# A hybrid encoder layer on one core: a column sum queued later, and the first half's final norm on GpSimd and ScalarE

## The chip, the cores and the metric

The kernel runs on one core of a Trainium2 chip. The metric is the device time of one execution in microseconds. The core's engines are TensorE (PE; its weight loads are PEld), VectorE (DVE), ScalarE (ACT), GpSimd (POOL) and SyncE (SP). Each engine takes its own instructions strictly in order, and an instruction that has to wait holds everything behind it in its queue. In this kernel all loads and stores are issued from SP's queue.

## The reference

One layer and a final norm on x of 2048 frames x 1024 channels, float32. What is computed, cut to its core:

```python
h = rmsnorm(x, norm_mix_w)
proj = h @ w_in                              # 1024 -> 5648 columns
y_a = u_b * causal_dwconv(u_c * u_h, w)      # short convolution, width 3
y_b = rmsnorm(ssd_scan(silu(conv4(xbc)), softplus(dt), ...) * silu(z))
x = x + concat(y_a, y_b) @ w_out             # 2048 -> 1024
h = rmsnorm(x, norm_mlp_w)
hid = square(relu(h @ w_up))                 # 1024 -> 4096
x = x + hid @ w_down                         # 4096 -> 1024
out = x * rsqrt(mean(x * x) + eps) * final_norm_w
```

## The kernel before

Channels lie on the 128 partitions, frames along the free dimension. A float32 operand is split into a rounded part and a remainder (`hi` and `lo`, both in TensorE's fp32r format), and each product is made of three matmuls: hi by hi, hi by lo, lo by hi. So every weight and every activation passes through one cast (ScalarE, L100 for weights, L368 for activations) and one subtraction (VectorE, L101 and L369).

The projections in, up and down use a two-by-two block scheme with seven products instead of eight: `b11, t1, t2, b21, t3, b22, t4`, in this order, one after the other (the function `chain`). A step of that order takes about 19 us. The products add up in PSUM: b11, t2, t3 and t4 in the tile px, t1 and b22 in py, b21 in pw. After t1, t2, b21, t3, b22 and t4 the sum so far is read out (in the down projection by L1109, which adds it to a result tile), and TensorE goes on into px for t3 only when VectorE has read t2's sum, and for t4 only when it has read t3's.

The scheme needs sums of weight blocks. `combine` (L246) makes them for the next step while the present one runs: from two raw tiles r0 and r1 it splits r0, makes s12 (its first half by the addition L252, its second by a subtraction L229), splits s12, makes s34 by two subtractions, splits s34, and splits half of r1. In the first half of the projection in, and in the MLP's first half, s12 and s34 are also stored, to be loaded again in the second half. The raw tiles come by DMA, the loads being issued at the start of a step.

The order in which an engine's instructions stand is not the program's order alone: a scheduler puts them in order by priority and by when it takes their operands to be ready. `tc.issue_after(ins)` puts all instructions of a block behind `ins` on its engine. `kept` tiles and raw activations share small pools: `raw` (tag `uraw`) has four buffers for the reloaded activations `rh` and for the tiles `lf` of the final norm.

The frames are worked in two halves of 1024. In the down projection the first half is done some steps before the second, and from there on `finish_first` makes its final norm beside the second half's matmuls: for each of two blocks of 512 frames it loads eight channel tiles in pairs (`lf`), squares each pair on ScalarE (L1232), adds the squares on VectorE (L1234, L1237), makes the inverse root (`parts`, `whole`, with a reciprocal at L184), loads the pairs again, multiplies each tile by its weight column and by the inverse root in one VectorE instruction (L1248), and stores the pair. It moves on by one such piece after the products b11, t2 and t3 of a step. The second half's norm at the kernel's end (`norm_out`) does two of its tiles per three on VectorE, and one with the weight on ScalarE (L1205) and the inverse root on GpSimd (L1206).

Of the kernel before, what the change touches and what calls it, by code (L numbers as in the profile page):

```python
# [40 lines left out]
def trunk(ctx: ExitStack, tc: tile.TileContext, x, w_in, w_dt, w_out, w_up, w_down, cvec, hrow, out):  # L41
# [56 lines left out]
    def split_w(raw, eng):  # L98
        hi, lo = wtile(raw.shape[-1])
        nc.scalar.copy(hi, raw)  # L100
        eng.tensor_tensor(out=lo, in0=raw, in1=hi.bitcast(F32), op=ALU.subtract)  # L101
        return hi, lo

    def split_src(src):
        k = src.shape[1]
# [105 lines left out]
    class Seven:  # L211
# [35 lines left out]
        def combine(self, r0, r1, kept=None):  # L247
            w = r0.shape[-1] // 2
            a, b = slice(0, w), slice(w, 2 * w)
            yield split_w(r0, nc.vector)  # L250
            s12 = self.sumtile("s12")[:, 0 : 2 * w]
            nc.vector.tensor_tensor(out=s12[:, a], in0=r1[:, a], in1=r1[:, b], op=ALU.add)  # L252
            self.sub(s12[:, b], s12[:, a], r0[:, a])
            if kept is not None:
                nc.sync.dma_start(kept[:, 0], s12)
            yield split_w(s12, nc.vector)
            s34 = self.sumtile("s34")[:, 0 : 2 * w]
            self.sub(s34[:, a], r0[:, a], r1[:, a])
            self.sub(s34[:, b], r0[:, b], s12[:, b])
            if kept is not None:  # L260
                nc.sync.dma_start(kept[:, 1], s34)
            yield split_w(s34, nc.vector)
            yield split_w(r1[:, b], nc.vector)

        def chain(self, groups, ws, ahead, evict, after):
# [615 lines left out]
    class Mlp(Seven):  # L881
# [336 lines left out]
        def finish_first(self):  # L1218

            for bb in range(NBB):  # L1220
# [9 lines left out]
                for d in range(0, KD, 2):  # L1230
                    t = load(d)
                    nc.scalar.activation(t, t, AF.Square)  # L1232
                    if d == 0:
                        nc.vector.tensor_tensor(out=acc, in0=t[:, 0], in1=t[:, 1], op=ALU.add)  # L1234
                    else:
                        for i in range(2):
                            nc.vector.tensor_tensor(out=acc, in0=acc, in1=t[:, i], op=ALU.add)  # L1237
                    yield
                st = self.rstd()
                st.parts(acc)  # L1240
# [4 lines left out]
                for d in range(0, KD, 2):  # L1245
                    t = load(d)
                    for i in range(2):
                        nc.vector.scalar_tensor_tensor(  # L1248
                            out=t[:, i], in0=t[:, i], scalar=col(C_NFIN, d + i), in1=r, op0=ALU.mult, op1=ALU.mult
                        )  # L1250
                    nc.sync.dma_start(out[bb, :, d : d + 2], t)
                    yield

# [488 lines left out]
```

## Time and profile before

| | |
|---|---|
| median of the runs shown | 2623.73 us (2623.39 to 2628.8, three runs) |
| the profiled execution | 2627.32 us, of which the span from first to last instruction is 2625.6 us |
| granted TensorE clock, mean | 0.997 |
| TensorE busy | 2601.6 us, 99% |
| VectorE busy | 1917.3 us, 73% |
| ScalarE busy | 1468.0 us, 56% |
| GpSimd busy | 58.1 us, 2% |

A busy time is the time in which the engine had an instruction under way. A wait row reads: who waited, for which instruction, total in microseconds, times, longest. A timeline row reads: start and duration in microseconds, engine, source line, operation, result and operands by the program's names, shapes; in square brackets how long the engine was idle before it, and what ended that. Lines of the order are lines of the program, not times. The program's stages follow each other: projection in to about 930 us, projection out with the scan beside it to about 1390, up projection to about 1980, down projection to about 2570, then the last products and the second half's norm.

### The profile page before, as it was taken

How to read it: one execution, taken by the hardware profiler on the slowest of the kernel's cores; microseconds unless marked ns; L12 is line 12 of the kernel's file. 1: busy time of each engine (PE TensorE's matmuls, PEld its weight loads, DVE VectorE, ACT ScalarE, POOL GpSimd, SP SyncE). 2: the span in 40 equal slices, each digit the busy share in tenths (PEclk: the TensorE clock that was granted, in tenths of full speed). 3: DMA queues.
4: the chain of work that ended last, by engine and by line, in shares of the span. 5: the costliest groups of instructions: out<-in, count | busy, mean ns of one | idle time of the engine just before them, and what ended most of it. 6: DMA issues, size and time to landing. Idle time of an engine off the chain costs nothing.

```text
span 2625.6 us, 33818 instructions
## 1 busy us (share of the span) xinstructions
PE 2601.6 (99%) x12139; PEld 2141.9 (82%) x12139; DVE 1917.3 (73%) x2631; ACT 1468.0 (56%) x2230; POOL 58.1 (2%) x99
## 2 busy tenths in 40 slices
PE   9999999999999999999999999999999999999998
PEld 7788888788888888888888888888888888888887
DVE  7877877777778777778677775744448887888985
ACT  7654345776667666768335555755556444444533
POOL 1010000000000000000000000000000000000001
PEclk9999999999999999999999999999999999999998
DMA  4545745644555578877656786765557654665762
GB/s 155 194 172 181 278 143 194 208 156 164 170 165 173 167 270 257 272 221 230 206 196 237 263 314 235 280 212 193 197 192 254 194 174 153 217 200 180 244 201 69
DMA packets 252169, 536.98 MB, mean 205 GB/s; under 512 B 26208, under 2 KB 93024, under 8 KB 252000
## 3 DMA queue, kind: packets, MB, share of 16 engines
q1 hardware_dynamic: 251856, 534.29, 61.1%
q8 instruction: 95, 1.56, 0.2%
q14 instruction: 74, 0.61, 0.1%
q10 hardware_dynamic: 144, 0.52, 0.1%
HBM read 354.89 MB, written 179.83 MB: 204 GB/s over the span
## 4 chain that ended last, share of the span: by engine, by line
PE 86%; DMA 5%; DVE 4%; ACT 3%; issue 2%; SPq 0%; POOL 0%; POOLq 0%; DVEq 0%; ACTq 0%
PE px L296 13%; PE px L297 13%; PE px L298 13%; PE py L296 6%; PE py L298 6%; PE py L297 6%; PE pm L113 4%; PE pm L114 4%; PE pm L115 4%; PE pw L296 3%; PE pw L298 3%; PE pw L297 3%; PE yd L1391 1%; PE yo L1388 1%; DMA ry<-yn_d 1%
## 5 line engine op out<-in xcount | busy, mean ns | idle before, releaser
L296 PE MATMUL px<-uh,whi 128*128 128x512 f32 x1672 | 655.7, 392 | 6.7 <-DVE res L1109 1.9
L298 PE MATMUL px<-uh,wlo 128*128 128x512 f32 x1672 | 651.4, 390 | 0.0
L297 PE MATMUL px<-ul,whi 128*128 128x512 f32 x1672 | 650.9, 389 | 0.0
L296 PEld LDWEIGHTS px<-uh,whi 128*128 128x128 f32 x1672 | 313.9, 188 | 80.8 <-DVE acc L1109 3.1
L101 DVE TENSOR_TENSOR wlo<-wraw,whi 128x512 fp32r<-128x512 f32 (+1 forms) x213 | 221.1, 1038 | 211.9 <-ACT whi L100 209.7
L298 PEld LDWEIGHTS px<-uh,wlo 128*128 128x128 f32 x1672 | 313.8, 188 | 66.0 <-issue 0.2
L297 PEld LDWEIGHTS px<-ul,whi 128*128 128x128 f32 x1672 | 314.0, 188 | 64.0
L100 ACT CAST whi<-wraw 128x1024 fp32r<-128x1024 f32 x214 | 193.9, 906 | 305.4 <-PE px L297 228.0
L100 ACT CAST whi<-s 128x1024 fp32r<-128x1024 f32 x210 | 219.9, 1047 | 228.4 <-PE py L297 95.0
L296 PE MATMUL py<-uh,whi 128*128 128x512 f32 x836 | 327.2, 391 | 1.3 <-ACT s L773 0.8
L298 PE MATMUL py<-uh,wlo 128*128 128x512 f32 x836 | 325.5, 389 | 0.0
L297 PE MATMUL py<-ul,whi 128*128 128x512 f32 x836 | 325.5, 389 | 0.0
L101 DVE TENSOR_TENSOR wlo<-s,whi 128x1024 fp32r<-128x1024 f32 x210 | 255.1, 1215 | 71.5 <-ACT whi L100 69.4
L113 PE MATMUL pm<-uh,whi 128*128 128x512 f32 (+1 forms) x648 | 251.6, 389 | 0.1
L114 PE MATMUL pm<-ul,whi 128*128 128x512 f32 (+1 forms) x648 | 248.2, 383 | 0.5 <-DVE ul L226 0.5
L115 PE MATMUL pm<-uh,wlo 128*128 128x512 f32 (+1 forms) x648 | 248.2, 383 | 0.0
L296 PEld LDWEIGHTS py<-uh,whi 128*128 128x128 f32 x836 | 156.9, 188 | 35.9 <-ACT s L773 1.3
L298 PEld LDWEIGHTS py<-uh,wlo 128*128 128x128 f32 x836 | 156.9, 188 | 32.7
L297 PEld LDWEIGHTS py<-ul,whi 128*128 128x128 f32 x836 | 157.0, 188 | 32.1
L368 ACT CAST uh<-rh 128x1024 fp32r<-128x1024 f32 (+1 forms) x128 | 120.4, 944 | 78.0 <-PE py L298 61.7
L296 PE MATMUL pw<-uh,whi 128*128 128x512 f32 x418 | 163.4, 391 | 0.0
L298 PE MATMUL pw<-uh,wlo 128*128 128x512 f32 x418 | 162.8, 389 | 0.0
(259 smaller groups left out, 3799.8 us busy)
## 6 DMA issues: line engine op xcount, KB each, us to landing
hid_d<-e SPq DMA_DIRECT2D x96, 512.0 KB, 3.9
rh<-hid_d SPq DMA_DIRECT2D x96, 512.0 KB, 4.3
wraw<-w_in SPq DMA_DIRECT2D x68, 512.0 KB, 3.9
wraw<-w_down SPq DMA_DIRECT2D x104, 256.0 KB, 3.7
wraw<-w_up SPq DMA_DIRECT2D x48, 512.0 KB, 4.1
dec<-rd_d SPq DMA_DIRECT2D x32, 512.0 KB, 5.7
wraw<-w_out SPq DMA_DIRECT2D x32, 512.0 KB, 5.0
x_d<-xt SPq DMA_DIRECT2D x64, 256.0 KB, 3.9
```

What stands on the lines that cost most here:

```text
L100: nc.scalar.copy(hi, raw)
L101: eng.tensor_tensor(out=lo, in0=raw, in1=hi.bitcast(F32), op=ALU.subtract)
L113: nc.tensor.matmul(out, whi, hi, start=(k == 0), stop=False)
L114: nc.tensor.matmul(out, whi, lo, start=False, stop=False)
L115: nc.tensor.matmul(out, wlo, hi, start=False, stop=(k == nk - 1))
L296: nc.tensor.matmul(p, hi, h[0], start=not seeded and k == 0, stop=False, **kw)
L297: nc.tensor.matmul(p, hi, h[1], start=False, stop=False, **kw)
L298: nc.tensor.matmul(p, lo, h[0], start=False, stop=(k == len(g) - 1), **kw)
L368: nc.scalar.copy(p[i][0], t)
L1388: nc.tensor.matmul(yo[:, j * L : (j + 1) * L], state[:, j * P : (j + 1) * P], cT, start=True, stop=True)
L1391: nc.tensor.matmul(yd[(i % 2) * 64 : (i % 2) * 64 + 64, (i // 2) * L : (i // 2 + 1) * L], byhead(t["xdt"])[:, i, :], t["dec"][:, i % 2 * 4 ...
```

## The change

Two parts. In `combine` the first instruction of s12 is queued behind the last instruction of the s34 split of the combination made before it (the first combination has none before it). In `finish_first` the additions of squares go from VectorE to GpSimd, and the one instruction that multiplied by weight column and inverse root becomes two: the column on ScalarE, the inverse root on GpSimd.

```diff
--- before.py
+++ after.py
@@ -98,8 +98,10 @@
     def split_w(raw, eng):
         hi, lo = wtile(raw.shape[-1])
         nc.scalar.copy(hi, raw)
-        eng.tensor_tensor(out=lo, in0=raw, in1=hi.bitcast(F32), op=ALU.subtract)
+        split["last"] = eng.tensor_tensor(out=lo, in0=raw, in1=hi.bitcast(F32), op=ALU.subtract)
         return hi, lo
+
+    split = {}
 
     def split_src(src):
         k = src.shape[1]
@@ -249,7 +251,9 @@
             a, b = slice(0, w), slice(w, 2 * w)
             yield split_w(r0, nc.vector)
             s12 = self.sumtile("s12")[:, 0 : 2 * w]
-            nc.vector.tensor_tensor(out=s12[:, a], in0=r1[:, a], in1=r1[:, b], op=ALU.add)
+            cut = split.get("third")
+            with tc.issue_after(cut.ins) if cut else nullcontext():
+                nc.vector.tensor_tensor(out=s12[:, a], in0=r1[:, a], in1=r1[:, b], op=ALU.add)
             self.sub(s12[:, b], s12[:, a], r0[:, a])
             if kept is not None:
                 nc.sync.dma_start(kept[:, 0], s12)
@@ -259,7 +263,9 @@
             self.sub(s34[:, b], r0[:, b], s12[:, b])
             if kept is not None:
                 nc.sync.dma_start(kept[:, 1], s34)
-            yield split_w(s34, nc.vector)
+            parts = split_w(s34, nc.vector)
+            split["third"] = split["last"]
+            yield parts
             yield split_w(r1[:, b], nc.vector)
 
         def chain(self, groups, ws, ahead, evict, after):
@@ -1231,10 +1237,10 @@
                     t = load(d)
                     nc.scalar.activation(t, t, AF.Square)
                     if d == 0:
-                        nc.vector.tensor_tensor(out=acc, in0=t[:, 0], in1=t[:, 1], op=ALU.add)
+                        nc.gpsimd.tensor_tensor(out=acc, in0=t[:, 0], in1=t[:, 1], op=ALU.add)
                     else:
                         for i in range(2):
-                            nc.vector.tensor_tensor(out=acc, in0=acc, in1=t[:, i], op=ALU.add)
+                            nc.gpsimd.tensor_tensor(out=acc, in0=acc, in1=t[:, i], op=ALU.add)
                     yield
                 st = self.rstd()
                 st.parts(acc)
@@ -1245,9 +1251,8 @@
                 for d in range(0, KD, 2):
                     t = load(d)
                     for i in range(2):
-                        nc.vector.scalar_tensor_tensor(
-                            out=t[:, i], in0=t[:, i], scalar=col(C_NFIN, d + i), in1=r, op0=ALU.mult, op1=ALU.mult
-                        )
+                        nc.scalar.mul(t[:, i], t[:, i], col(C_NFIN, d + i))
+                        nc.gpsimd.tensor_tensor(out=t[:, i], in0=t[:, i], in1=r, op=ALU.mult)
                     nc.sync.dma_start(out[bb, :, d : d + 2], t)
                     yield
```

The scheduler moves more than the named instructions. In the pieces below the line numbers of the changed kernel are 2 to 6 higher for the same code: L252 and L256 are the addition of s12, L229 and L231 subtractions, L369 and L375 the remainders of activations, L1109 and L1115 the reading of a product's sum.

VectorE in a step of the down projection, before (s_20039 is s12 of the next step, s_19932 is s34 of the combination before it; the px reading at this place is that of t3, the py reading that of b22):

```order
L101 TENSOR_TENSOR wlo<-s_19893,whi 128x1024
L252 TENSOR_TENSOR s_20039<-wraw 128x512
L1109 TENSOR_TENSOR res<-px,res 128x512
L229 TENSOR_TENSOR s_20039<-s_20039,wraw 128x512
L369 TENSOR_TENSOR ul_19940<-rh,uh_19939 128x1024
L1109 TENSOR_TENSOR acc<-py,acc 128x512
L101 TENSOR_TENSOR wlo<-s_19932,whi 128x1024
L369 TENSOR_TENSOR ul_19963<-rh,uh_19962 128x512
```

and in the changed kernel:

```order
L101 TENSOR_TENSOR wlo<-s_19893,whi 128x1024
L1115 TENSOR_TENSOR res<-px,res 128x512
L375 TENSOR_TENSOR ul_19940<-rh,uh_19939 128x1024
L1115 TENSOR_TENSOR acc<-py,acc 128x512
L101 TENSOR_TENSOR wlo<-s_19932,whi 128x1024
L375 TENSOR_TENSOR ul_19963<-rh,uh_19962 128x512
L256 TENSOR_TENSOR s_20039<-wraw 128x512
L1115 TENSOR_TENSOR acc<-px,acc 128x512
L101 TENSOR_TENSOR wlo<-wraw,whi 128x512
```

The addition of s12 stands five instructions later, behind both readings and the s34 split.

VectorE in the projection in, first half, where the inverse root of a norm is made (facc), before:

```order
L101 TENSOR_TENSOR wlo<-s_1925,whi 128x1024
L252 TENSOR_TENSOR s_2071<-wraw 128x512
L184 RECIPROCAL facc<-facc 128x512
L776 TENSOR_TENSOR eb<-px,s_1892 128x512
L776 TENSOR_TENSOR ea<-py,s_1906 128x512
L750 TENSOR_TENSOR eb<-eb,cc 128x512
L750 TENSOR_TENSOR ea<-ea,cc 128x512
L101 TENSOR_TENSOR wlo<-s_1967,whi 128x1024
L750 TENSOR_TENSOR eb<-px,cc 128x512
L101 TENSOR_TENSOR wlo<-wraw,whi 128x512
L229 TENSOR_TENSOR s_2071<-s_2071,wraw 128x512
```

and in the changed kernel:

```order
L101 TENSOR_TENSOR wlo<-s_1925,whi 128x1024
L186 RECIPROCAL facc<-facc 128x512
L782 TENSOR_TENSOR eb<-px,s_1892 128x512
L782 TENSOR_TENSOR ea<-py,s_1906 128x512
L756 TENSOR_TENSOR eb<-eb,cc 128x512
L756 TENSOR_TENSOR ea<-ea,cc 128x512
L101 TENSOR_TENSOR wlo<-s_1967,whi 128x1024
L256 TENSOR_TENSOR s_2071<-wraw 128x512
L756 TENSOR_TENSOR eb<-px,cc 128x512
L101 TENSOR_TENSOR wlo<-wraw,whi 128x512
```

The addition of s12 has gone from ahead of the reciprocal to behind the s34 split (wlo of s_1967).

ScalarE in the up projection, first half, where squares for the next norm (lx) stand between the readings of a step, before:

```order
L930 ACTIVATE e_12162<-e_12162 128x512
L396 ACTIVATE lx<-lx 128x1024
L923 COPY s_12334<-px 128x512
L923 COPY s_12358<-py 128x512
L100 CAST whi<-wraw 128x1024
L923 COPY s_12372<-px 128x512
```

and in the changed kernel:

```order
L936 ACTIVATE e_12162<-e_12162 128x512
L929 COPY s_12334<-px 128x512
L929 COPY s_12358<-py 128x512
L100 CAST whi<-wraw 128x1024
L929 COPY s_12372<-px 128x512
L100 CAST whi<-s_12397 128x1024
L935 ACTIVATE e_12318<-e_12318 128x512
L936 ACTIVATE e_12318<-e_12318 128x512
L935 ACTIVATE e_12320<-e_12320 128x512
L936 ACTIVATE e_12320<-e_12320 128x512
L100 CAST whi<-s_12439 128x1024
L402 ACTIVATE lx<-lx 128x1024
```

A square (L396, L402) that stood ahead of the copies of px and py now stands behind them, and behind the casts and activations that follow.

## The prediction

> **What bounds the kernel now.** I read the page first, then the waits of TensorE and VectorE, then the timeline around each wait of TensorE.
>
> ```profile
> span 2625.6 us, 33818 instructions
> PE 2601.6 (99%) x12139; PEld 2141.9 (82%) x12139; DVE 1917.3 (73%) x2631; ACT 1468.0 (56%) x2230; POOL 58.1 (2%) x99
> ...
> PE px L296 <- DVE res L1109: 1.9, 2, 1.0
> PE px L296 <- DVE eb L776: 1.6, 2, 0.9
> ...
> PE px L296 <- DVE acc L1109: 1.0, 3, 0.5
> PE px L296 <- ACT s L923: 0.9, 1, 0.9
> ```
>
> TensorE is busy for 99% of the span; what can be won without touching its matmuls are short waits, in the last four rows 5.4 us over eight of them (total, times, longest). So the whole question is which of these go and which new ones come. One of them, seen closely, in the down projection (start, duration, what, idle before it):
>
> ```profile
> 2183.53 0.69 DVE L252 TENSOR_TENSOR s<-wraw 128x512 f32<-128x512 f32 x1 [2.29 <-DMA wraw<-w_down]
> 2184.14 0.68 DVE L1109 TENSOR_TENSOR acc<-px,acc 128x512 f32<-128x512 f32 x1
> ...
> 2181.30 0.39 PE L298 MATMUL px<-uh,wlo 128*128 128x512 f32 x1
> 2184.02 0.39 PE L298 MATMUL py<-uh,wlo 128*128 128x512 f32 x1
> 2184.88 0.50 PE L296 MATMUL px<-uh,whi 128*128 128x512 f32 x1 [0.47 <-DVE acc L1109]
> 2185.22 0.40 PE L297 MATMUL px<-ul,whi 128*128 128x512 f32 x1
> ```
>
> From 2181.30 to 2184.02 twelve matmuls start, 0.227 us apart. The t3 product ends at 2181.30 and leaves its sum in px; TensorE computes the b22 product into py meanwhile and then wants px back for t4. VectorE should have emptied px (L1109, reading px), but in its queue the first column sum of the next step's weights (L252) stands ahead and waits 2.29 us for weights that are still on their way. The px read is late, and TensorE stands for 0.47 us. The price is higher than the gap: from 2184.02 to 2185.22 are 1.20 us for two steps of 0.227, so 0.75 us are lost, 0.28 more than the gap. The others of the kind:
>
> ```profile
> 2356.63 0.69 DVE L252 TENSOR_TENSOR s<-wraw 128x512 f32<-128x512 f32 x1 [2.65 <-DMA wraw<-w_down]
> 2357.97 0.50 PE L296 MATMUL px<-uh,whi 128*128 128x512 f32 x1 [0.83 <-DVE res L1109]
> 2414.75 0.69 DVE L252 TENSOR_TENSOR s<-wraw 128x512 f32<-128x512 f32 x1 [2.20 <-DMA wraw<-w_down]
> 2416.09 0.50 PE L296 MATMUL px<-uh,whi 128*128 128x512 f32 x1 [0.38 <-DVE acc L1109]
> 2106.60 0.69 DVE L252 TENSOR_TENSOR s<-wraw 128x512 f32<-128x512 f32 x1 [1.78 <-DMA wraw<-w_down]
> 2534.65 0.69 DVE L252 TENSOR_TENSOR s<-wraw 128x512 f32<-128x512 f32 x1 [3.60 <-DMA wraw<-w_down]
> ...
> DVE s L252 <- DMA wraw<-w_down: 26.5, 19, 3.6
> ```
>
> Wait minus gap is 1.82 us each time (2.29 - 0.47, 2.65 - 0.83, 2.20 - 0.38), and a wait of 1.78 us leaves no row among TensorE's waits. So **VectorE may be 1.82 us late at this place of a step**, and everything above is paid by TensorE. The sum waits 19 times in this stage, and 16 of them cost nothing; the longest, at 2534.65, stands where px has been read already.
>
> **Part one, the later sum.** In the changed order the sum stands behind the px read of t3, a cast difference of 128x1024, the py read of b22, the s34 difference and the 128x512 difference of t4's operand. By the time VectorE is there, 4 us later, the weights of all three rows above have landed (2184, 2357, 2415, against px reads at about 2182, 2355 and 2413). So the three stalls go: gaps 0.47 + 0.83 + 0.38, with 0.28 each, 2.52 us. The step also gains tolerance, since the 0.61 us from the start of L252 to the next row leave the place: 2.43 us instead of 1.82. Nothing is late from it: the 128x1024 split that reads this sum is a step's half away, and the last readers of both raw weight tiles keep their places, so the loads on SP's queue start as before.
>
> In the first half the same sum stands ahead of a reciprocal, and in the MLP's first half a square on ScalarE stands ahead of two copies out of PSUM:
>
> ```profile
> 222.14 0.69 ACT L183 ACTIVATE facc<-pss,cv 128x512 f32<-128x512 f32 x1
> 223.85 0.69 DVE L252 TENSOR_TENSOR s<-wraw 128x512 f32<-128x512 f32 x1 [1.76 <-DMA wraw<-w_in]
> 224.46 3.34 DVE L184 RECIPROCAL facc<-facc 128x512 f32<-128x512 f32 x1
> 227.72 0.63 DVE L776 TENSOR_TENSOR eb<-px,s 128x512 f32<-128x512 f32 x1
> 228.40 0.50 PE L296 MATMUL px<-uh,whi 128*128 128x512 f32 x1 [0.93 <-DVE eb L776]
> ...
> 1398.46 1.06 ACT L396 ACTIVATE lx<-lx 128x1024 f32<-128x1024 f32 x1 [1.62 <-DMA lx<-x_d]
> 1400.04 0.50 PE L296 MATMUL px<-uh,whi 128*128 128x512 f32 x1 [0.94 <-ACT s L923]
> ```
>
> At 223.85 the sum's wait and its 0.61 us leave the queue ahead of the reciprocal, so the px read moves up by about 1.6 us (the reciprocal's input leaves ScalarE at 222.14 + 0.69, and 1.63 us after that the reciprocal starts): 0.93 + 0.28 = 1.21 us. At 1398.46 the square that waited for its load now stands behind the two copies: 0.94 + 0.28 = 1.22 us. Part one together: 2.52 + 1.21 + 1.22 = 4.95 us. Bounds: 5.4 us if two of the small waits left go too; below, 2.5 if the reordered first halves (where additions of squares and scaled blocks change places too) bring as much as they lose.
>
> **Part two, the final norm of the first half.** It takes 2 + 12 additions and 16 products off VectorE:
>
> ```profile
> L1248 DVE SCALAR_TENSOR_TENSOR lf<-lf,cv,facc x16: 734/742/751, 2428.7 to 2520.8; 128x512 f32<-128x512 f32 x16
> L1237 DVE TENSOR_TENSOR facc<-facc,lf x12: 678/686/693, 2383.0 to 2473.5; 128x512 f32<-128x512 f32 x12
> 2375.00:2520.00 145.00, 143.60 (x631) 117.63 (x630) 130.19 (x164) 68.24 (x79) 0.00 (x0) 1.00 0.68 221
> 2508.27 0.75 DVE L1248 SCALAR_TENSOR_TENSOR lf<-lf,cv,facc 128x512 f32<-128x512 f32 x1 [1.40 <-DMA lf<-fin_d]
> 2513.68 0.50 PE L296 MATMUL px<-uh,whi 128*128 128x512 f32 x1 [1.02 <-DVE res L1109]
> ```
>
> That is 16 x 0.742 + 14 x 0.686 = 21.5 us (the two first additions taken like the other twelve) of VectorE's 130.19 us (third pair of the windows row, after TensorE's two; then ScalarE, GpSimd). One stall hangs on it directly: VectorE waits 1.40 us for the tile it is to scale, and 5 us later the px read is late: 1.02 + 0.28 = 1.30 us.
>
> What it adds is 16 products by a column on ScalarE and 30 two-input operations on GpSimd. The end of the kernel runs both on the same shape:
>
> ```profile
> L1205 ACT ACTIVATE res<-res,cv 128x512 f32<-128x512 f32 x1 | 0.7, 727 | 0.0
> 2597.45 1.29 POOL L1206 TENSOR_TENSOR res<-res,facc 128x512 f32<-128x512 f32 x1 [1682.69 <-ACT facc L201]
> 2598.70 2.55 POOL L1206 TENSOR_TENSOR acc<-acc,facc 128x512 f32<-128x512 f32 x2
> 2599.98 1.54 DVE L1171 TENSOR_TENSOR acc<-acc,sq 128x256 f32<-128x256 f32 x1
> 2601.45 0.41 DVE L1190 TENSOR_TENSOR acc<-pm,acc 128x256 f32<-128x256 f32 x1
> ```
>
> ScalarE: 16 x 0.727 = 11.6 us on 68.24 of 145, 55% full. Its new operations wait for the loads in its queue, and casts stand behind them, but those casts are for the step after, several products away. I take 0; with that cover gone it would be one 1.40 us wait per load, as on VectorE now. The output stores on SP wait for GpSimd where they waited for VectorE; refills and weights stand behind them. GpSimd has nothing else to do, so a pair takes 2.6 us from its data, against 1.4 us plus VectorE's queue: 0 as well, with one 1.3 us delay per pair as the upper price.
>
> GpSimd: 30 x 1.29 = 38.7 us, off the path itself, but the last rows show what it does to VectorE. While GpSimd ran from 2598.70 to 2601.25, a VectorE addition of two 128x256 SBUF tiles took 1.54 us; the addition behind it, with one input in PSUM, took 0.41. So a VectorE operation with two SBUF inputs stands until GpSimd's is over. How much of the 38.7 us falls on such work: in the same 145 us the lines for ul (L369), wlo (L101), and the column sums (L229, L252) are busy for
>
> ```profile
> 2375.00:2520.00 145.00, 32.01 (x30) 1.00 0.68 221
> 2375.00:2520.00 145.00, 32.20 (x30) 0.00 (x0) 1.00 0.68 221
> 2375.00:2520.00 145.00, 13.85 (x21) 1.00 0.68 221
> 2375.00:2520.00 145.00, 4.83 (x7) 1.00 0.68 221
> ```
>
> 32.01 + 32.20 + 13.85 + 4.83 = 82.9 us, 57%. Bounds: 0 (GpSimd always in the gaps) and 38.7 us; I take 57% of it, 22 us, as those operations are met by chance. VectorE then loses 22 us and is relieved of 21.5: its fill stays where it is, at 90%. What changes is where the delay falls. A pair on GpSimd holds VectorE for at most 2 x 1.29 = 2.58 us, against the tolerance of 2.43 us: 0.15 + 0.28 = 0.43 us where a pair falls fully ahead of a px read. I take two of the 14 pairs, 0.9 us. The Trainium skill, SBUF — State Buffer, section Who interferes with whom, says that a VectorE instruction with two SBUF inputs contends with a GpSimd instruction that reads SBUF, since they share a read port that is held as a lock. The trace agrees (1.54 us). By that rule alone, without gaps, the whole 38.7 us would count, which is the third rival.
>
> **Sum.** In the profiled execution: 2627.32 - 4.95 - 1.30 + 0.9 = 2622.0 us, 5.3 us less (of its 2627.32 us, 1.7 lie outside the span). The median of the runs shown is 2623.73, 3.6 us below this execution. All stalls counted hang on when a transfer lands, and some of these 3.6 us may be just such waits; then as little as 1.7 us of the gain is left. Between 5.3 and 1.7 I take 4.2, nearer to the profile since 3.6 us spread over the span would leave most: **2619.5 us**.
>
> **Rivals.** *All of it comes, and no new stall:* 4.95 + 1.30 = 6.25 us, 2617.5 us. For it: the waits are seen one by one, and GpSimd's blocks fall under the tolerance. Against it: the 3.6 us between profile and median. *Nothing to be seen:* without the profiler the three down-projection waits stay under 1.82 us, as most of the 19 do in the trace already, and the stalls of the first halves only move: 1.21 + 1.22 - 2 x 0.9 for two new waits of the same size = 0.6 us, 2623.1 us. *GpSimd holds VectorE where no tolerance is left:* at 100% the 38.7 us replace 21.5, VectorE needs 147.4 us in a stage of 145 and falls behind for good; behind each 3.34 us reciprocal its queue runs late as it is. A pair then costs 2.58 - 1.37 = 1.2 us, with 0.28, 1.5 us. From four such pairs of the 14 on (6.0 us) part one's gain is gone; with seven it is 10.4 - 4.95 = 5.4 us slower, 2629.2 us. Against it: VectorE ran without a stall of TensorE behind the reciprocal of 2423 us.
>
> **Chances.** About 0.2%, 5.2 us, is what can be told from no change here. Forecast (a gain of 1.7 to 5.2 us): 0.44. All of it (over 5.2 us): 0.34. Nothing to be seen (from 1.7 us gain to 5.2 us loss): 0.15. GpSimd's hold: 0.07. So faster 0.34, same 0.59, slower 0.07. The range takes the full gain with a microsecond beyond it, 2616.5, and upward the cases without gain and the first stalls of the hold, 2625.5; the forecast's own is 2618.5 to 2622.
>
> **What would show it.** Right: no wait of px for a L1109 behind a column sum; the column sum's own wait for w_down near 0 instead of 26.5 us; no gap at 228 and 1400; VectorE's busy time in 2375 to 2520 near 130 us although 30 instructions are gone, as the ul and wlo rows there are stretched. Wrong: TensorE waiting for L1109 while GpSimd works; ul or wlo waiting for casts that stand behind the new ScalarE products; SP's queue waiting for GpSimd with weights or refills late behind it; or VectorE's mean durations unchanged, which would mean that the block is no lasting one.

## The result, and the profile after

| | before | after |
|---|---|---|
| median | 2623.73 us (2622.12 to 2629.32, five runs) | 2636.2 us (2632.35 to 2637.91, five runs) |
| the profiled execution | 2627.32 us, span 2625.6 us | 2636.2 us, span 2634.2 us |
| granted TensorE clock, mean | 0.997 | 0.996 |

The ratio is 1.0042, interval 1.0031 to 1.0053: the change makes the kernel slower, by 12.5 us between the medians. The forecast was 2619.5 us, in a range of 2616.5 to 2625.5.

The waits of TensorE over the whole span, longest first, and two rows of the page (share of the span):

```profile
span 2634.2 us, 33878 instructions
PE 2602.6 (99%) x12139; PEld 2143.6 (81%) x12139; DVE 1912.6 (73%) x2601; ACT 1477.0 (56%) x2246; POOL 106.7 (4%) x129
...
PE px L302 <- ACT pw L309: 7.5, 2, 7.2
PE px L302 <- DVE acc L1115: 3.1, 4, 1.3
PE px L302 <- DVE res L1115: 1.8, 1, 1.8
```

The longest wait before was 1.2 us. Now there is one of 7.2 us, and its releaser is a new name: L309, ScalarE's copy of px into pw, which starts the pw sum of a product with the b11 sum.

**Part one did what was forecast.** The matmul that stood at 2357.97 us before, behind the stall of 0.83 us, now starts without one:

```profile
2353.82 0.39 PE L302 MATMUL px<-uh,whi 128*128 128x512 f32 x1
...
DVE s L256 <- DMA wraw<-w_down: 1.2, 1, 1.2
```

It is the same matmul counted from the start of the program: 4.15 us earlier. The five stalls that part one was to remove can be followed in this way, from the matmul before each to the fifth behind it (228.40, 1400.04, 2184.88, 2357.97 and 2416.09 us of before): the lead grows there by 1.20, 1.23, 0.77, 1.13 and 0.66 us, 4.99 together, where 1.21, 1.22, 0.75, 1.11 and 0.66 were forecast. In between it drifts by up to some 2 us to either side. The second row, from VectorE's waits, is what is left of the column sum's waits for w_down, 1.2 us in one place instead of 26.5 in 19.

**The loss lies in the stage of the first half's norm.** From 2357.97 of before to its 2540.13, the same stretch of matmuls takes 15.6 us longer (2353.82 to 2551.60), so a lead of 4.15 us becomes a lag of 11.47. Six waits of TensorE stand in it: 1.08, 0.35, 1.33, 7.20, 0.47 and 1.78 us, 12.2 together. The largest, in the timeline (the rows come from four engines, so their times don't run through):

```profile
2459.78 3.50 POOL L1243 TENSOR_TENSOR facc<-facc,lf 128x512 f32<-128x512 f32 x2 [3.85 <-ACT lf L1238]
...
2463.31 0.80 SPq L1232 DMA_DIRECT2D lf<-fin_d  x2
...
2461.01 0.61 ACT L100 CAST whi<-wraw 128x512 fp32r<-128x512 f32 x1
2467.40 1.06 ACT L1238 ACTIVATE lf<-lf 128x1024 f32<-128x1024 f32 x1 [5.78 <-DMA lf<-fin_d]
2468.36 0.58 ACT L309 COPY pw<-px 128x512 f32<-128x512 f32 x1
...
2469.00 0.79 PE L302 MATMUL px<-uh,whi 128*128 128x512 f32 x1 [7.20 <-ACT pw L309]
```

Read upward: TensorE wants px back and waits for the copy L309. That copy stands in ScalarE's queue behind the square L1238, which waits 5.78 us for its lf tile. The load was issued at 2463.31, 0.03 us after GpSimd's additions on an earlier lf tile ended (2459.78 + 3.50): SP had waited for the buffer (lf and the reloaded activations have four together). And GpSimd began those additions late because it had itself waited 3.85 us for a square. It is a loop over few buffers: load (4 us from issue to square), square, additions (3.5 us), buffer free, next load. The wait of 1.78 us, later, comes by another way from the same source. The matmul that waits is the one that stood 1.02 us at 2513.68 before:

```profile
2515.06 1.34 ACT L1254 ACTIVATE lf<-lf,cv 128x512 f32<-128x512 f32 x2 [5.12 <-DMA lf<-fin_d]
2516.30 1.04 ACT L100 CAST whi<-wraw 128x1024 fp32r<-128x1024 f32 x1
...
2517.37 2.13 DVE L101 TENSOR_TENSOR wlo<-wraw,whi 128x1024 fp32r<-128x1024 f32 x1 [1.68 <-ACT whi L100]
...
2522.81 0.68 DVE L1115 TENSOR_TENSOR res<-px,res 128x512 f32<-128x512 f32 x1
...
2523.55 0.50 PE L302 MATMUL px<-uh,whi 128*128 128x512 f32 x1 [1.78 <-DVE res L1115]
```

Here the cast of the next weights is behind ScalarE's product L1254 and its 5.12 us wait for a load; VectorE waits 1.68 us for the cast; its subtraction takes 2.13 us where the same takes 1.22 us otherwise; and the px read behind it is late. In this second chain lateness and the hold of GpSimd on VectorE both take part, which is why the trace alone does not settle the cause.

After two of the waits the matmuls go at half pace for a while (length, busy time of PE, PEld, DVE, ACT, POOL, then the granted clock, DMA share, GB/s):

```profile
2469.00:2474.50 5.50, 5.50 (x14) 4.35 (x15) 3.10 (x3) 1.35 (x2) 2.08 (x2) 0.56 0.50 171
2474.50:2480.00 5.50, 5.50 (x25) 4.53 (x25) 5.09 (x5) 3.47 (x4) 2.82 (x2) 1.00 0.36 114
2525.00:2529.00 4.00, 4.00 (x12) 3.08 (x12) 2.75 (x5) 0.17 (x1) 0.00 (x0) 0.57 0.99 299
```

Starts are 0.427 us apart instead of 0.227. The twelve steps from 2469.00 take 5.10 us instead of 2.72, the nine from 2525.04 take 3.65 instead of 2.04: 2.4 and 1.6 us lost. So the 15.6 us add up: 12.2 of waits, 1.4 for restarting after five of them (0.28 each), 4.0 of half pace, less the 2.0 us of two stalls that before had in this stretch (0.38 and 1.02, with 0.28 each). The span grows by only 8.6 us. In the last stage the execution of before was granted half the clock (0.50) from 2594.95 to 2598.36 us and again from 2615.43 on, this one only from 2627.47 on, behind its last matmul; the 2.9 us between 11.47 and 8.6 are put down to this, not measured by themselves.

What the norm's engines wait for between 2375 and 2540 us (SP's queue first, then ScalarE), and a group of VectorE's instructions (count, then busy time and mean ns of one, then the idle time before them and what ended it). First three rows of before, the stores, the squares and the same group:

```profile
SPq L1251 <- DVE lf L1248: 10.1, 8, 2.0
...
ACT lf L1232 <- DMA lf<-fin_d: 12.2, 6, 4.4
...
L369 DVE TENSOR_TENSOR ul<-rh,uh 128x1024 fp32r<-128x1024 f32 x25 | 30.4, 1216 | 0.2 <-ACT uh L368 0.2
```

and in the changed kernel:

```profile
SPq L1256 <- POOL lf L1255: 35.5, 8, 7.3
...
SPq L1232 <- POOL facc L1243: 13.0, 4, 3.6
...
SPq L1033 <- POOL facc L1243: 3.6, 1, 3.6
...
ACT lf L1254 <- DMA lf<-fin_d: 23.4, 10, 5.1
ACT lf L1238 <- DMA lf<-fin_d: 22.2, 6, 5.8
...
L375 DVE TENSOR_TENSOR ul<-rh,uh 128x1024 fp32r<-128x1024 f32 x23 | 34.2, 1487 | 10.8 <-ACT uh L374 10.8
```

SP waits for GpSimd 35.5 us with the stores (10.1 for VectorE before), 13.0 with the lf loads and 5.5 with loads of reloaded activations (3.6 and, not shown, 1.9 for L1240), 54.0 together; ScalarE waits 45.6 us for lf (12.2 before). The last row shows the hold: the remainders of activations take 1487 ns on the mean instead of 1216. Over all VectorE instructions from 2370 to 2545 us the hold can be added up: each one's duration, less the median of the same operation and shape in three traces without GpSimd work there (before, act_dve, bare), is 15.0 us together. This sum, the **lengthening**, is used below as the dose of the hold.

### The profile page after: what moved, and what is told of

Read it like the earlier page. It is cut to its first block, busy times and chain, and to the rows that moved or that the text cites. A ratio compares the mean times of both kernels' runs of the same rounds, so it can differ in the third digit from the quotient of the medians.

```text
span 2634.2 us, 33878 instructions
## 1 busy us (share of the span) xinstructions
PE 2602.6 (99%) x12139; PEld 2143.6 (81%) x12139; DVE 1912.6 (73%) x2601; ACT 1477.0 (56%) x2246; POOL 106.7 (4%) x129
## 4 chain that ended last, share of the span: by engine, by line
PE 86%; DMA 4%; DVE 4%; ACT 3%; issue 2%; POOL 1%; SPq 0%; POOLq 0%; DVEq 0%; ACTq 0%
PE px L302 13%; PE px L303 13%; PE px L304 13%; PE py L302 6%; PE py L303 6%; PE py L304 6%; PE pm L115 5%; PE pm L116 4%; PE pm L117 4%; PE pw L302 3%; PE pw L304 3%; PE pw L303 3%; DMA lf<-fin_d 1%; PE yd L1396 1%; PE yo L1393 1%
## 5 line engine op out<-in xcount | busy, mean ns | idle before, releaser
L375 DVE TENSOR_TENSOR ul<-rh,uh 128x1024 fp32r<-128x1024 f32 (+1 forms) x128 | 144.8, 1135 | 42.5 <-ACT uh L374 42.3
```

The costliest lines, as they stand in the source:

```text
L375: nc.vector.tensor_tensor(out=p[i][1], in0=t, in1=p[i][0].bitcast(F32), op=ALU.subtract)
```

## The experiments

Two theories. **Q, the queues:** GpSimd's results come late; SP, whose loads and stores stand in one queue, waits for them, so the next lf tiles are late; ScalarE waits for those with the px to pw copy, the casts of weights and the cast of the norm's sum behind it. **L, the hold:** while GpSimd reads SBUF, a VectorE instruction with two SBUF inputs stands, and the splits come late without anything waiting for GpSimd.

All ratios are to the kernel before, measured beside it on the same chip. A ratio of 0.0010 is 2.6 us. A difference between two of them has an interval of about 3.5 us to either side, nearer 5 with norm_only, ahead or hold. "The whole change" is 1.0042.

| kernel | ratio | interval | median, us |
|---|---|---|---|
| sum_only: later sum alone | 0.9986 | 0.9976 to 0.9995 | 2619.46 |
| norm_only: norm moved, sum as before | 1.0088 | 1.0073 to 1.0103 | 2646.41 |
| adds_pool: later sum, only the additions moved | 1.0017 | 1.0007 to 1.0027 | 2626.44 |
| prods_pool: later sum, only the products moved | 1.0030 | 1.0019 to 1.0041 | 2629.84 |
| ahead: whole change, loads a piece earlier | 1.0041 | 1.0025 to 1.0057 | 2636.87 |
| sum_ahead: later sum, loads a piece earlier | 0.9970 | 0.9957 to 0.9983 | 2618.15 |
| act_dve: later sum, column products on ScalarE, nothing on GpSimd | 0.9976 | 0.9966 to 0.9986 | 2618.01 |
| act_ahead: act_dve, loads a piece earlier | 0.9978 | 0.9969 to 0.9987 | 2617.54 |
| hold: GpSimd dummies, misplaced | 1.0096 | 1.0080 to 1.0112 | 2652.07 |
| hold2, hold4: act_dve and GpSimd dummies | 1.0002, 1.0018 | 0.9992 to 1.0011, 1.0009 to 1.0028 | 2624.0, 2628.71 |
| pw_first: whole change, ScalarE's norm work behind the px to pw copy | 1.0013 | 1.0004 to 1.0023 | 2627.38 |
| pw_parts: and the sum's parts a piece later | 1.0000 | 0.9991 to 1.0009 | 2623.47 |
| mended: and the loads a piece earlier | 1.0029 | 1.0017 to 1.0041 | 2629.32 |
| bare: act_dve with most of the norm left out | 0.9987 | 0.9978 to 0.9996 | 2617.8 |
| bare_hold, bare_wide: bare and GpSimd dummies | 0.9985, 0.9998 | 0.9976 to 0.9995, 0.9987 to 1.0008 | 2618.61, 2621.83 |
| bare_late: bare, slots and sums wait for GpSimd | 1.0033 | 1.0022 to 1.0043 | 2631.97 |

### The two parts, and the two halves of the second

sum_only takes part two back (additions and product on VectorE, as before). norm_only takes part one back:

```diff
-            cut = split.get("third")
-            with tc.issue_after(cut.ins) if cut else nullcontext():
-                nc.vector.tensor_tensor(out=s12[:, a], in0=r1[:, a], in1=r1[:, b], op=ALU.add)
+            nc.vector.tensor_tensor(out=s12[:, a], in0=r1[:, a], in1=r1[:, b], op=ALU.add)
```

> Only the later column sum; the final norm of the first half stays on VectorE. Theory A (the two parts are independent; the whole loss is the norm's): the waits at 228, 1400, 2185, 2358 and 2416 us go as in the changed kernel, where the matmul of 2358 us came 4.2 us earlier than before; the wait at 2514 us stays. So 2618 to 2620 us, 4 to 5 us under before. Rival B (the later sum itself upsets the down projection's queues beside the norm): within 2 us of before or slower.

> Only the move of the norm to GpSimd and ScalarE, the column sum queued as before. Theory A: the loss of the changed kernel, 12.5 us, plus the 4 to 5 us that the later sum brings: 2639 to 2642 us. Rival B (the two need each other to lose): clearly under the changed kernel, 2624 to 2632 us.

The later sum alone is faster by 0.0014, 3.7 us. The norm alone is slower by 0.0088, 23 us, more than either theory expects, so with the norm moved the later sum saves 12 us (0.0088 - 0.0042). VectorE's waits in norm_only between 2375 and 2540 us show one difference:

```profile
DVE s L254 <- DMA wraw<-w_down: 17.1, 6, 3.9
```

The weights come later when the norm is moved, up to 3.9 us after VectorE is there. But how the 12 us come about is not shown: of the 15.7 us that TensorE waits in this stretch of norm_only, only 1.11 stand right behind such a wait of the column sum, and the four longest waits (5.39, 2.87, 2.69 and 2.16 us) stand behind casts of ScalarE's that came late. The late weights are also the first sign that SP's queue, through which the weights are loaded, runs late.

adds_pool has the product on VectorE in one instruction again, prods_pool the additions:

> Later sum, and only the 14 additions on GpSimd; the 16 products stay on VectorE. Theory Q (queues: ScalarE's squares and products wait for reloads, the reloads stand on SP behind stores that wait for GpSimd, and the copy of px to pw stands behind on ScalarE): the stores no longer wait for GpSimd and ScalarE has no products, so the 7 us stall with its slow matmuls behind it goes and 2619 to 2625 us come out. Rival L (GpSimd's hold on VectorE's two-input work costs by GpSimd's time): 14 of 30 operations, half of the 17 us lost, so 2626 to 2629 us.

> Later sum, and only the 16 products on ScalarE and GpSimd; the 14 additions stay on VectorE. Theory Q: most of the loss is here, 2629 to 2636 us, with ScalarE waiting for reloads at its products and the px to pw copy late. Rival L: 16 of 30 operations, half of the loss, 2626 to 2629 us, and waits of TensorE for VectorE's readings rather than for ScalarE's copy.

Over the later sum alone, the additions on GpSimd cost 0.0031 (8.1 us), the products 0.0044 (11.5 us), both 0.0056 (14.7 us). Each half costs by itself, so it isn't one bad place. The pair does not decide between the theories: for the additions Q expected less (2619 to 2625 us) and the median, 2626.44, lies in L's range; for the products it lies in Q's (2629.84, L had 2626 to 2629).

### The loads a piece earlier, and ScalarE without GpSimd

```diff
-                for d in range(0, KD, 2):
-                    t = load(d)
+                nxt = load(0)
+                yield
+                for d in range(0, KD, 2):
+                    t = nxt
                     nc.scalar.activation(t, t, AF.Square)
...
+                    if d + 2 < KD:
+                        nxt = load(d + 2)
                     yield
```

and the same in the second loop. act_dve differs from the whole change only in the engine of the additions and of the product with the root:

```diff
-                        nc.gpsimd.tensor_tensor(out=t[:, i], in0=t[:, i], in1=r, op=ALU.mult)
+                        nc.vector.tensor_tensor(out=t[:, i], in0=t[:, i], in1=r, op=ALU.mult)
```

> The changed kernel with one thing moved: each lf load of the first half's final norm is issued one piece earlier (the first of each block in a step of its own, and the next behind the work on the present one), so that ScalarE should find the tile there. GpSimd does the same 30 operations of 1.29 us. Theory Q (queues: ScalarE waits for lf loads that SP issues late because the slot waits for GpSimd, and the product's px to pw copy and the cast of the next weights stand behind that wait): ScalarE's waits for lf between 2375 and 2530 fall from 45.6 us to under 15, the 7.20 us stall goes, and the time to 2622 to 2629. Theory L (GpSimd's operations stretch VectorE's two-input ones, 1.22 us to 2.3 us, and that alone makes the weights' splits and the accumulation late): nothing of the hold changes, 2632 to 2637.

> The later column sum alone (norm on VectorE as before), with the lf loads one piece earlier. Q: what is left of ScalarE's waits for lf (12.2 us before the change) goes with the 1.5 us stall near 2504: 2617 to 2619. L: no GpSimd work in it, so no difference from the later sum alone, 2619.5 within 1.

> The later column sum, the norm's products by the column weight on ScalarE as in the changed kernel, but the products by the reciprocal root and the adds on VectorE: nothing on GpSimd. If ScalarE's 16 products of 0.73 us and the wait for their load are enough by themselves to delay the px to pw copy and the casts (Q without GpSimd): 2623 to 2628. If it takes GpSimd, by its late release of the slots or by its hold: 2619 to 2621, as the later sum alone.

ahead gains nothing, which spoke for L. But the experiment did not take the queues' waits away: ScalarE's waits for lf fall only from 45.6 to 30.8 us, and SP's for GpSimd are 55.7 us where they were 54.0 (2375 to 2540 us; 2.3 us for L1242 are not shown):

```profile
SPq L1261 <- POOL lf L1260: 33.0, 8, 6.1
...
SPq L1033 <- POOL facc L1245: 10.7, 3, 3.6
SPq L1232 <- POOL facc L1245: 9.7, 3, 3.7
...
ACT lf L1240 <- DMA lf<-fin_d: 19.0, 6, 4.7
...
ACT lf L1259 <- DMA lf<-fin_d: 11.8, 6, 4.7
```

L1033, the loads of the reloaded activations, wait for GpSimd more than twice as long as in the changed kernel, 13.0 us instead of 5.5 (10.7 instead of 3.6 in the rows for L1245 and L1243). They share the four buffers with lf, and an lf tile taken a piece earlier holds one the longer. An earlier load doesn't help where the buffer is what comes late.

act_dve is 2618.0 us, as fast as anything here. ScalarE has the 16 additional products, waits for lf, and TensorE hardly notices (2375 to 2540 us):

```profile
PE px L302 <- DVE acc L1115: 0.4, 2, 0.2
ACT lf L1238 <- DMA lf<-fin_d: 15.0, 7, 3.9
...
ACT lf L1254 <- DMA lf<-fin_d: 10.9, 5, 3.9
```

So ScalarE's new work and 25.9 us of waits for lf cost nothing that could be seen as long as VectorE frees the buffers. Without GpSimd there is no loss; what remains open is whether its lateness or its hold makes it.

### The hold alone

The first try put operations of no use on GpSimd, on constants, into the later sum alone, each group started by a 128x1 copy of a constant on ScalarE.

> The later column sum alone, norm on VectorE, plus work of no use on GpSimd at the places where the changed kernel has its own: for each of the 30 operations four of 128x128 on two constants, each group started by a 128x1 copy on ScalarE, so that no load, no slot and no store ever waits for GpSimd. Only its hold on VectorE is added. L: most of the 16.7 us between the later sum alone (2619.5) and the changed kernel (2636.2) comes back, 2630 to 2637. Q: 2620 to 2624.

2652.07 us, but it says nothing of the question: a copy of a constant depends on nothing, and the scheduler put all of them, and the GpSimd work with them, near 1430 us, in the MLP, where ScalarE's copies waited for GpSimd (1390 to 1560 us):

```profile
ACT tick L1228 <- POOL tri L1230: 26.1, 11, 5.3
...
PE px L302 <- ACT s L929: 25.7, 2, 24.3
```

One stall of 24.3 us came of it, behind four such waits in a row. It does show that ScalarE waiting for GpSimd can be expensive. In hold2 and hold4 the copy takes what ScalarE has just written, so that the work runs where the changed kernel's does, on top of act_dve:

```diff
                     nc.scalar.activation(t, t, AF.Square)
+                    hold(t[:, 0, 0:1], 1 if d == 0 else 2)
...
                         nc.scalar.mul(t[:, i], t[:, i], col(C_NFIN, d + i))
+                        hold(t[:, i, 0:1], 1)
...
+            def hold(x, n):
+                tick = self.up.tile([P, 1], F32, tag="tick", name="tick", bufs=8)
+                nc.scalar.copy(tick, x)
+                for i in range(2 * n):
+                    nc.gpsimd.tensor_tensor(
+                        out=tri, in0=tri, in1=ident if i else tick.to_broadcast([P, P]), op=ALU.add
+                    )
```

hold4 has 4 * n there.

> Later column sum, column products on ScalarE, the other products and the adds on VectorE (2618.0 as measured), plus work of no use on GpSimd: for each of the 30 operations of the changed kernel two of 128x128 on constants, about 1.19 us beside 1.29 us, each group started by a 128x1 copy on ScalarE from what ScalarE has just written, so that it runs where the changed kernel's does. No slot, load or store waits for GpSimd. Theory L (the hold on VectorE's two-input work alone costs the time): 2628 to 2636, with VectorE's splits stretched from 1.22 us and the stalls at the px reads back; since VectorE also keeps the adds and products, rather more than the 16.7 us is possible. Theory Q (it takes the loads and stores that wait for GpSimd): 2618 to 2622.

> As hold2 with four of 128x128 for each operation, 2.4 us: twice the hold. L: about twice the loss of hold2, 2638 to 2656. Q: 2618 to 2624, no dependence on the dose.

Against act_dve they cost 0.0026 and 0.0042, 6.8 and 11.0 us: more than Q expects, growing with the dose, less than L expects. But VectorE keeps the norm's work here and is busy 151.6 of the 165 us from 2375 to 2540 in hold2, so this is the price of a hold on a full VectorE (lengthening 8.8 us in hold2, 17.8 in hold4). In the changed kernel it is busy 133.0.

### The queues, one after another

pw_first is the whole change with ScalarE's squares and column products queued behind the px to pw copy; pw_parts also issues the cast and the remainder of the norm's sum, which wait for GpSimd's last addition, a piece later; mended also has the loads a piece earlier, as above.

```diff
-                        nc.scalar.copy(pm[gi]["w"], pm[gi]["x"])
+                        split["pw"] = nc.scalar.copy(pm[gi]["w"], pm[gi]["x"])
...
-                    nc.scalar.activation(t, t, AF.Square)
+                    with tc.issue_after(split["pw"].ins):
+                        nc.scalar.activation(t, t, AF.Square)
...
-                        nc.scalar.mul(t[:, i], t[:, i], col(C_NFIN, d + i))
+                        with tc.issue_after(split["pw"].ins):
+                            nc.scalar.mul(t[:, i], t[:, i], col(C_NFIN, d + i))
```

and for pw_parts

```diff
                 st = self.rstd()
+                yield
                 st.parts(acc)
                 yield
-                yield
                 r = st.whole(acc)
```

> The changed kernel, with ScalarE's work on the loads of the final norm (squares and column products) kept behind the px to pw copy of the product in which it is written, so that no such copy can stand behind a wait for a load. Q in the narrow form (the copy behind the load makes the stalls): the 7.2 us and 2 smaller pw stalls and a half-clock stretch of 2.4 us go, 2625 to 2629. L: the copies are not the cause but where it shows; 2632 to 2638.

> As pw_first (2627.4), and the cast and the subtraction of the sum's parts, which wait for GpSimd's last add with px reads and casts queued behind them, issued one place later. If these waits count: 2624 to 2626. If what is left is the hold alone: 2626.5 to 2628.5.

> As pw_parts, and the lf loads one piece earlier: all three waits taken away, GpSimd's 30 operations left. If the queues made nearly all of the loss: 2618 to 2621. If the hold has a share of its own of about 6 us, as on the busier VectorE: 2623 to 2627.

The order on ScalarE alone gives back 0.0029, 7.6 us; with the parts later it is 0.0042, 11.0 us of the 14.7, and the kernel is where before was. (The second step by itself, 3.4 us, is not clear of the interval.) GpSimd does all it did, and its hold is the same: the remainders of activations take 1482 ns (1487 in the changed kernel), and the lengthening is 15.1 us (15.0). Yet TensorE's waits in this stretch are down from 12.2 to 4.9 us:

```profile
L375 DVE TENSOR_TENSOR ul<-rh,uh 128x1024 fp32r<-128x1024 f32 x25 | 37.0, 1482 | 15.6 <-ACT uh L374 15.5
...
PE px L302 <- DVE acc L1115: 4.9, 5, 2.6
```

No wait for L309 is left, though SP still waits 43.9 us for GpSimd and ScalarE 28.2 for lf: the waits are there, but what TensorE needs no longer stands behind them. mended is a miss for both expectations: with the loads a piece earlier on top, it is slower than pw_parts by 0.0029 (7.6 us). ScalarE's waits for lf between 2375 and 2540 us, 28.2 us of loads in pw_parts, are down to 11.3 here, but another wait for GpSimd has grown, that of the cast of the norm's sum (2.8 us, once, in pw_parts):

```profile
ACT ahi L177 <- POOL facc L1246: 9.1, 2, 4.5
...
2405.71 0.62 ACT L177 CAST ahi<-facc 128x512 fp32r<-128x512 f32 x1 [4.54 <-POOL facc L1246]
...
2412.67 0.50 PE L302 MATMUL px<-uh,whi 128*128 128x512 f32 x1 [1.38 <-DVE acc L1115]
```

So in mended one wait went and another of the same kind grew. TensorE stands for 1.38 us some 7 us after the one shown; how much of the 7.6 us is due to these waits was not measured.

### Hold and lateness apart

bare leaves out 12 of the norm's 14 additions and its 16 products by the inverse root, from act_dve: VectorE then is as free as in the changed kernel (busy 129.7 us of the 165), and GpSimd has nothing. On it, bare_hold has the operations of hold2; bare_wide has one 128x512 addition for each of the changed kernel's 30 operations, into a buffer of its own, so that nothing waits for it; bare_late makes slots, stores and the sum's parts wait for GpSimd with hardly any reading of two inputs:

```diff
+            def hold(scr, t, at):
+                for i in at:
+                    x = t[:, i, 0:1]
+                    nc.gpsimd.tensor_copy(scr[:, 0:1], x)
+                    for _ in range(2):
+                        nc.gpsimd.memset(scr, 0.0)
+                    nc.gpsimd.tensor_tensor(out=x, in0=x, in1=scr[:, 0:1], op=ALU.add)
```

called behind each square and each column product.

> Later column sum; of the norm only loads, ScalarE's squares and column products, one add per block, the reciprocal root and the stores are left: the other 12 adds and the 16 products by the root are left out, so VectorE has about 17 us less and GpSimd nothing. Measures the base for bare_hold: 2616 to 2619.

> bare plus the work of no use on GpSimd of hold2 (60 operations of 128x128, about 36 us alone), with VectorE as free as in the changed kernel. L: at least 6 us over bare, 2623 to 2630. Q (the hold costs only where VectorE has no room, and the loss in the changed kernel is waits in queues): under 3 us over bare.

> As bare_hold (norm's 12 adds and 16 products by the root left out), but the work of no use on GpSimd is one 128x512 addition for each of the changed kernel's 30 operations, into a buffer that nothing else uses. VectorE's splits should stretch to 1.4 to 1.5 us on the mean, as in the changed kernel. If the hold by itself costs time with VectorE as free as there: 4 us or more over bare (2617.8), 2622 to 2630. If it costs nothing until something waits for GpSimd: 2617 to 2620.

> bare, with the load slots, the stores and the sum's parts made to wait for GpSimd: for each of the 30 operations it copies one column, sets a spare 128x512 buffer to zero twice and adds one column back, 1.5 to 2 us estimated from its copies and settings of this kernel, with only the one-column addition reading two inputs. Lateness without the hold. If the queues' waits for GpSimd are what costs: 5 us or more over bare, 2623 to 2634. If it takes the hold: 2617 to 2621.

Timed, against bare: bare_hold -0.0002 (nothing), bare_wide +0.0011 (2.9 us by the ratios, 4.0 by the medians, not surely different from none), bare_late +0.0046 (12.1 us by the ratios, 14.2 by the medians). The same group of VectorE's in bare, bare_hold, bare_wide and bare_late, one fence each, between 2375 and 2540 us, and TensorE's waits in all but bare_hold:

```profile
L375 DVE TENSOR_TENSOR ul<-rh,uh 128x1024 fp32r<-128x1024 f32 x25 | 30.5, 1221 | 5.7 <-ACT uh L374 5.6
...
PE px L302 <- DVE acc L1115: 3.0, 2, 2.7
PE px L302 <- ACT pw L309: 0.8, 1, 0.8
```

```profile
L375 DVE TENSOR_TENSOR ul<-rh,uh 128x1024 fp32r<-128x1024 f32 x25 | 32.1, 1283 | 5.0 <-ACT uh L374 5.0
```

```profile
L375 DVE TENSOR_TENSOR ul<-rh,uh 128x1024 fp32r<-128x1024 f32 x25 | 33.9, 1358 | 4.9 <-ACT uh L374 4.9
...
PE px L302 <- DVE acc L1115: 4.8, 4, 1.9
```

```profile
L375 DVE TENSOR_TENSOR ul<-rh,uh 128x1024 fp32r<-128x1024 f32 x23 | 28.1, 1220 | 6.8 <-ACT uh L374 6.8
...
PE px L302 <- DVE acc L1115: 5.9, 3, 3.4
PE px L302 <- ACT pw L309: 3.8, 2, 2.1
PE px L302 <- DVE res L1115: 2.3, 1, 2.3
...
ACT lf L1263 <- DMA lf<-fin_d: 28.1, 9, 6.0
ACT lf L1248 <- DMA lf<-fin_d: 23.3, 7, 6.5
```

bare_late has no stretched split at all (1220 ns, as bare) and yet the whole picture of the changed kernel: ScalarE waits 51.4 us for lf, TensorE for L309 and for px reads, 12.0 us together. bare_wide has the stretched splits and no such picture. The traces are single executions, that of bare its slowest (2624.79 us); its wait of 2.7 us shows that late loads can now and then cost something without GpSimd.

The doses are not those of the changed kernel. In bare_late GpSimd is busy 57.4 us between 2375 and 2540 us (45.2 in the changed kernel). The hold is weaker in both other runs: splits of 1283 and 1358 ns (1487 there), a lengthening of 4.2 us in bare_hold and 10.0 in bare_wide (15.0 there, 0.3 in bare_late). An estimate in proportion: the 2.9 us of bare_wide would be 4.4 us at the full lengthening, the 12.1 us of bare_late 9.5 us at the GpSimd time of the changed kernel. The shares are estimates, but their order agrees with pw_parts, where the full hold leaves 3.7 us.

So lateness in the queues makes most of the loss: it costs 12.1 us without the hold, at a somewhat larger dose, and freeing what TensorE needs from standing behind it gives back three quarters with the hold in place. How the 3.7 us divide that pw_parts still has over the later sum alone, between the hold and SP's waits for GpSimd that stay there, is open.

None of act_dve, act_ahead and sum_ahead can be told from the others; they beat before by 5.8 to 7.9 us (ratios 0.9970 to 0.9978), and each leaves GpSimd out.

## Why the prediction was wrong

**Part one, 4.95 us: right.** The lead is 4.15 us at 2353.82 in one profiled execution, and 3.7 us (1.3 to 6.3) in the timed runs of the later sum alone. The column sum's waits went as told, and at the five stalls the lead grows by 4.99 us. That the later sum would be worth 12 us with the norm moved was not foreseen.

**Part two, ScalarE, "I take 0": the step that failed, together with the next.** "Those casts are for the step after, several products away" was true of most casts, but two things stand in the same queue for which TensorE waits at once: the px to pw copy after b11, and, by way of VectorE's subtraction and the px read behind it, the cast of the first weights. Neither was priced. The upper price, one 1.40 us wait per load, was taken from how late VectorE's loads were before; measured waits are up to 5.8 us, since the lateness is made by the change itself. act_dve shows that the 0 holds where the buffers are freed on time, so the error isn't ScalarE's 11.6 us of work. With these waits in place, queueing the copy and the sum's parts clear of them (pw_parts) gives back 11 of 14.7 us.

**Part two, stores and SP, "0 as well, with one 1.3 us delay per pair as the upper price": failed.** GpSimd's pair takes 2.6 to 4.6 us instead of VectorE's 1.4, and it begins only behind ScalarE's product. SP waits for it up to 7.3 us at a time, with all loads behind. The 1.3 us were the difference of two durations, but with a load, a square and the additions in a loop over shared buffers every piece's delay is the next one's start. This loop was not drawn. Lateness alone costs 12.1 us in bare_late. The prediction's own list of signs of being wrong has both paths, casts behind ScalarE's products and SP waiting for GpSimd; they were given no chance of their own, and the only clearly slower rival was the hold, at 0.07.

**Part two, GpSimd's hold, 0.9 us: the mechanism right, the sizes off.** Splits of 2.13 and 2.30 us instead of 1.22 are in the trace. VectorE loses 15 us to it where 22 were expected. The Trainium skill, SBUF — State Buffer, section Who interferes with whom, says that a GpSimd instruction that only writes does not contend with a VectorE instruction of two SBUF inputs: the trace of bare_late agrees (1220 ns beside GpSimd's zero settings). The price to the kernel is 2.9 us, not told from none, at two thirds of the lengthening with VectorE as free as here (4.4 us in proportion), and 6.8 us where VectorE is full. The third rival, 2629.2 us, had the sign, by luck, with the wrong mechanism: the hold is not what decides.

**The stall at 2513.68, 1.30 us gained: failed.** The same matmul stands at 2523.55 in the changed kernel and waits longer, 1.78 us instead of 1.02. The wait for the lf load has only moved from VectorE's queue to ScalarE's. In act_dve, where ScalarE's products wait for loads too but the buffers are freed on time, this matmul does not wait. (Nor does it in sum_only, where another one stands 1.51 us, so the place of such a stall is not fixed.)

VectorE's busy time "near 130 us" from 2375 to 2520 says little: it is 115.6 us there, since less of the work falls into that window, and 133.0 us for about the same work (649 matmuls, 631 before) in the stretch to 2540. VectorE has room; it idles behind casts.

The range failed with the sign: the two zeros' upper prices, a wait of 1.3 to 1.4 us per load or pair, went into neither the sum nor the range, whose upper end stands for no gain and the first stalls of the hold. And they were prices of single waits, not of a loop.

## What to carry to other kernels

When work moves to a slower engine, price the buffer it frees before its busy time: follow the loop load, compute, free, next load through every in-order queue, and list what stands behind each wait, the short copies first of all. A load issued earlier didn't help here (ahead, mended), where it takes a buffer from another stream. Where work must be on the slow engine, queue what waits for it behind the copies that the fast engine needs.

## What the runs showed of the hardware

A short idle time can cost the clock. After the wait of 7.20 us, and after one of only 1.78 us, TensorE was granted about half its clock (0.56 and 0.57) for some 5 and 3.6 us. In bare_late a wait of 2.13 us was followed by matmuls of 0.63 us each, while none followed one of 2.27 us, nor one of 3.34 us in prods_pool (granted clock 1.00 in the 10 us from 2512.85 on). The Trainium skill, TensorE: Matmul & The Clock Gate, section What's actually happening, says that the gate falls back after an idle window of about 3.4 us that runs freely; that a shorter wait does it and a longer one does not agrees with a free-running window, but waits of 1.78 and 2.13 us are shorter than the one it names.
